# An encoder kernel: the DRAM sums of the second value set, begun in the first layer's second branch half and issued one per 22 matmul steps instead of 15

## The chip, the cores and the metric

The kernel runs on one core of a Trainium2 chip. A core has five engines with a queue of instructions each: TensorE (PE: matmuls; PEld: their weight loads), VectorE (DVE), ScalarE (ACT), GpSimd (POOL) and SyncE (SP). Data move between DRAM and the on-chip memory by 16 DMA engines, which all queues share; here SyncE and GpSimd issue nearly all transfers. The metric is the device time of one execution in microseconds. Lower is better.

## The reference

A two-layer encoder over 272 tokens (16 learned ones and 256) with 2048 channels, in float32. Cut to what matters:

```python
for i in range(DEPTH):                                   # 2 layers
    h = _rmsnorm(h_stream, norm_mix[i])
    proj = h @ w_in[i]                                   # q | k | v | f | ga | gf
    ...
    a_br = attn @ w_attn_br[i]                           # attention branch
    s_br = fr.reshape(B, L, FOURIER_WIDTH) @ w_four[i]   # Fourier branch
    merged = g_attn * a_br + g_four * s_br               # sigmoid gates
    h_stream = h_stream + merged @ w_out[i]
    h2 = _rmsnorm(h_stream, norm_ffn[i])
    up = h2 @ w_up[i]
    u_gate = _dwconv3_centred(up[..., :D_FF], w_conv[i], b_conv[i])
    u_val = up[..., D_FF:]
    h_stream = h_stream + (jax.nn.silu(u_gate) * u_val) @ w_down[i]
return h_stream[:, N_META:]
```

## The kernel before

**Weights come in chunks.** Every weight matrix is read in chunks of 512 KB (128 partitions, 4 tiles of 256 columns). `order` lists all matmul groups in the order in which TensorE runs them, and `chunks` their chunks. `load_raw` (L233) issues one chunk's load on SyncE's queue into a `raw` buffer; there are four (`RAW`, L231). `split_w` (L270) splits a chunk into a rounded high part `wh`, on ScalarE (L277), and the rest `wl`, on VectorE (L279), three buffers each. A matmul with float32 accuracy is then three matmuls: high weights with the high and the low part of the activations, low weights with the high part (L348 to L350). `advance` (L245) issues loads up to four chunks ahead of the newest chunk that is to be split, and splitting runs two chunks ahead of TensorE (`LOOK`).

**Steps.** `group` (L322) runs one group: two output tiles of 128 channels, 2 to 11 chunks. After every second pair of weight tile and output tile, so four times a chunk, it calls `step` (L290), which lets one piece of other work be emitted between the matmuls, and `pump` (L257), which emits one pending split. `four_group` (L364) does the same for the s groups, whose two chunks take eight steps together.

**Branch halves.** Each layer computes the gated branches in two halves of 1024 channels. `BRANCH_ORDER` (L68) sets the order of the groups: ga and gf are the gate projections (16 steps each), s is the Fourier branch and a the attention branch (8 steps each). The second half's order is s4 a4 ga5 gf5 s5 a5 ga6 gf6 s6 a6 ga7 gf7 s7 a7. After each half come eight groups of the output projection (ps_o, 8 steps each). In the first layer an s chunk is first folded by `fold_w` (L264): VectorE writes sums and differences of its tiles into `wpm`, of which there is one buffer, and the split works from that (L267). In the second layer these folds come ready from DRAM (`fw`).

**What the second layer's feed-forward stage needs.** It computes part of the value projection and of the down projection by products of sums (fewer multiplications at the price of sums of weight tiles). The sums of weights lie in DRAM: `fv[0]` and `fv[1]` for two value sets, `ft` for the down projection. They are made in two ways. `prepare` (L509) runs in the first layer's feed-forward stage: GpSimd loads tiles, VectorE adds them, GpSimd stores them; it makes `fw`, `fv[0]` and `ft`. `weight_sums` (L549) makes `fv[1]` without VectorE, by transfers from DRAM to DRAM on GpSimd's queue: a plain copy of 1 MB into `fv[1]`, then a transfer that adds a second 1 MB to it (`accum_op=ALU.add`, called accumulating below). There are four kinds of sums with four blocks each, so 16 plain and 16 accumulating transfers; within a kind the order is copy 0, copy 1, add 0, copy 2, add 1, copy 3, add 2, add 3. Kind 1 copies what kind 0 made, and kind 3 adds what kind 1 made.

**When these transfers are issued.** `slow` (L288) holds a counter, the generator `weight_sums` and a period. While the period is not 0, each unforced `step` takes one off the counter; at 0 the counter is set to the period and the generator issues its next transfer. Before the transfer GpSimd copies one element of the newest `wl` (the `tick`, L554), so that the transfer isn't issued before that chunk was split. GpSimd executes its queue in order, and its few other instructions stand in the same queue, among them the power function of the norm statistics (`tok`, L489) and the loads and stores of `prepare`. The period is 15 from the fifth group (gf0) of the second layer's first half on.

Of the kernel before, what the change touches and what calls it, by code (L numbers as in the profile page):

```python
# [154 lines left out]
def encoder_kernel(ctx, tc, xT, params, consts, bmat, cfold, csign, w_fl, w_f64c, w_in, w_abr, w_four, w_f64, w_out, w_up, w_down, w_vn, w_dn, w_dt, out):  # L155
# [129 lines left out]
    def push(gen, wait=0):  # L285
        shadow.append([wait, gen])

    slow = [0, None, 0]  # L288
# [22 lines left out]
    def drain():  # L311
        while shadow:
            step(True)
# [42 lines left out]
    def split_w64(l, i):  # L356
        r = wp.tile([64, MG * P], F32, tag="r64", name="r64", bufs=1)
        nc.sync.dma_start(r, w_f64[l, i])
        w = wp.tile([96, MG * P], F32R, tag="w64", name="w64", bufs=2)
        nc.scalar.copy(w[0:64], r)  # L360
        nc.vector.tensor_tensor(w[64:96], r[32:64], w[32:64].bitcast(F32), op=ALU.subtract)
        return w
# [142 lines left out]
    def norm_in(m, goff):  # L505
        norm_split(m, goff)
        norm_sum(m)

    def prepare(pool):  # L509
        tt = lambda *v, **kw: tc.keep_in_program_order(nc.vector.tensor_tensor(*v, **kw))  # L510
        dma = lambda *v: tc.keep_in_program_order(nc.gpsimd.dma_start(*v))
        tile_ = lambda n: pool.tile([P, CW, MG * P], F32, tag="ws", name=n, bufs=7)
        folds = [(w_fl[k], k) for k in range(KT)] + [(w_four[1, j, c], KT + 2 * j + c) for j in range(NG) for c in range(2)]
        sums = []
        for s_, f, wd, nq in ((0, fv[0], w_vn[0], NV), (len(VSETS), ft, w_dn, NQ)):
            for k in range(nq):
                sums += [(wd[h, nq * e + k], (s_, f, q, k)) for h, e, q in ((0, 0, 0), (1, 0, 2), (1, 1, 1), (0, 1, 3))]

        def fold(held, n, j):
            a, o = held[n], tile_(f"wo{n}")  # L520
            for q, op in ((0, ALU.add), (1, ALU.subtract)):
                for c in range(2):
                    half = (lambda t_, e: t_[:, 2 * c:2 * c + 2, e * P:(e + 1) * P]) if j < KT else (lambda t_, e: t_[:, 2 * e + c])
                    tt(half(o, q), half(a, 0), half(a, 1), op=op)
                    yield 1
            dma(fw[j], o)

        def sum_up(held, n, s_, f, q, k):
            x, y = held[n], held[n + (1, -2, 1, -1)[q]]
            for c in (0, 2):  # L530
                tt(x[:, c:c + 2], x[:, c:c + 2], y[:, c:c + 2], op=ALU.add)
                yield 1
            dma(f[q, k], x)
            ready_sums.add((s_, q, k))

        for jobs, ahead, work in ((folds, 2, lambda h, n, to: fold(h, n, to)), (sums, 4, lambda h, n, to: sum_up(h, n, *to))):
            held = {}
            for n in range(len(jobs) + ahead):
                if n < len(jobs):
                    held[n] = tile_(f"wi{n}")  # L540
                    dma(held[n], jobs[n][0])
                left = 7 - n % 4 // 3
                if n >= ahead:
                    for v in work(held, n - ahead, jobs[n - ahead][1]):
                        left -= v
                        yield v
                yield left
# [56 lines left out]
    for l in range(DEPTH):  # L604
        last = l == DEPTH - 1
# [5 lines left out]
        with tc.tile_pool(name=f"mix{l}", bufs=1) as mp:  # L611
# [557 lines left out]
            def gate(kind, i):  # L1169
                ps = group((l, kind, i), xr(lo), W)  # L1170
                th = rt("th")
                boff = 2 * KT * l + (0 if kind == "ga" else KT)
                for m in range(MG):
                    u = th[:, m, lo:T]
                    nc.vector.tensor_tensor(u, ps[m][:, :W], rstdB[:, lo:T], op=ALU.mult)
                    bcol = bgh[:, boff + 2 * i + m:boff + 2 * i + m + 1]
                    nc.scalar.activation(u, u, AF.Tanh, bias=bcol, scale=0.5)
                return th

            tha, thf, w64s = {}, {}, []  # L1180
            for half in range(2):
                mH = mL = None
                for n_, (kind, i) in enumerate(BRANCH_ORDER[half]):
                    if last and (half or n_ >= 4):
                        slow[2] = 15
                    j = i - 4 * half
                    if kind == "ga":
                        tha[i] = gate("ga", i)
                    elif kind == "gf":
                        w64s.append(split_w64(l, i))  # L1190
                        thf[i] = gate("gf", i)
                    elif kind == "s":
                        def s_evac(m, ps, th=thf[i]):
                            e, o = (mp.tile([P, TH], F32, tag=t, name=t) for t in ("se", "so"))
                            for a, p_ in ((e, ps[0]), (o, ps[1])):
                                nc.scalar.copy(a, p_[:, TH:2 * TH])
                                nc.vector.tensor_tensor(a, p_[:, :TH], a, op=ALU.add)  # L1197
                            sp = mp.tile([P, T], F32, tag="sp", name="sp", bufs=2)
                            nc.vector.tensor_tensor(sp[:, 0:TH], e, o, op=ALU.add)
                            nc.vector.tensor_tensor(sp[:, TH:T], e[:, T - TH:0:-1], o[:, T - TH:0:-1], op=ALU.subtract)  # L1200
                            t_ = th[:, m, lo:T]
                            nc.vector.scalar_tensor_tensor(t_, t_, 1.0, sp[:, lo:T], op0=ALU.add, op1=ALU.mult)

                        four_group((l, "s", i), fr, x64, w64s.pop(0), s_evac)
                    else:
                        if mH is None:
                            drain()
                            mHf = mp.tile([P, AHn], F32R, tag="aH", name="mH")
                            mLf = mp.tile([P, ALn], F32R, tag="aL", name="mL")
                            mH = mHf[:, :8 * T].rearrange("p (k t) -> p k t", k=8)  # L1210
                            mL = mLf[:, :8 * T].rearrange("p (k t) -> p k t", k=8)
                        ps = group((l, "a", i), lambda kt: (qH[kt // 4][:, kt % 4, lo:T], qL[kt // 4][:, kt % 4, lo:T]), W)
                        for m in range(MG):
                            k = 2 * j + m
                            t_, h_ = tha[i][:, m, lo:T], mH[:, k, lo:T]
                            nc.vector.scalar_tensor_tensor(t_, t_, 1.0, ps[m][:, :W], op0=ALU.add, op1=ALU.mult)
                            nc.vector.tensor_tensor(t_, t_, thf[i][:, m, lo:T], op=ALU.add)
                            nc.scalar.copy(h_, t_)
                            nc.vector.tensor_tensor(mL[:, k, lo:T], t_, h_.bitcast(F32), op=ALU.subtract)
                for mg in range(8):  # L1220
                    ps = group((l, "o", half, mg), lambda kt: (mH[:, kt, lo:T], mL[:, kt, lo:T]), W)
                    for m in range(MG):
                        mt = 2 * mg + m
                        nc.vector.scalar_tensor_tensor(XT[:, mt, lo:T], ps[m][:, :W], 0.5, XT[:, mt, lo:T], op0=ALU.mult, op1=ALU.add)
                        if half == 1:
                            norm_in(mt, P_NF + l * KT)


        with tc.tile_pool(name=f"ffn{l}", bufs=1) as fp:
            hold = {}  # L1230
            push(norm_stats(hold), 8)
            if not last:
                push(prepare(fp), 8)
            def conv_gate(i):
                ps = group((l, "ug", i), xr(lo), W)
# [327 lines left out]
```

## Time and profile before

| what | us |
|---|---|
| median of 3 runs | 2531.81 |
| lowest and highest of them | 2531.63, 2534.08 |
| the profiled execution | 2533.09 |
| its span, from the first instruction to the last | 2531.2 |

The profile is of one execution. Its page gives busy times by engine, a chain of work that ended last, and groups of instructions; the trace behind it can be asked for single instructions, for busy times in stretches of the span, for what an engine waited for, and for the time from a DMA's issue to its landing. Names such as ps_gf<-xHL,wh say what an instruction writes and reads, L348 is a line of the kernel. Matmuls overlap one another, so PE counts as busy nearly always, and its idle time counts more than its share.

The main stages in this trace, by their first instructions: the first layer's second branch half runs from about 370 to 540 us, its feed-forward stage to about 1320, and the 32 transfers of `weight_sums` are issued from 1502 to 1843, in the second layer's branch halves. The second layer's feed-forward stage follows to the end.

### The profile page before, as it was taken

How to read it: one execution, taken by the hardware profiler on the slowest of the kernel's cores; microseconds unless marked ns; L12 is line 12 of the kernel's file. 1: busy time of each engine (PE TensorE's matmuls, PEld its weight loads, DVE VectorE, ACT ScalarE, POOL GpSimd, SP SyncE). 2: the span in 40 equal slices, each digit the busy share in tenths (PEclk: the TensorE clock that was granted, in tenths of full speed). 3: DMA queues.
4: the chain of work that ended last, by engine and by line, in shares of the span. 5: the costliest groups of instructions: out<-in, count | busy, mean ns of one | idle time of the engine just before them, and what ended most of it. 6: DMA issues, size and time to landing. Idle time of an engine off the chain costs nothing.

```text
span 2531.2 us, 47928 instructions
## 1 busy us (share of the span) xinstructions
PE 2517.9 (99%) x18848; PEld 2434.5 (96%) x18848; DVE 1985.4 (78%) x3151; ACT 1343.3 (53%) x1921; POOL 205.9 (8%) x393
## 2 busy tenths in 40 slices
PE   9999999999999999999999999999999999999999
PEld 8999999999999999999999999999988889998887
DVE  7687866778878667888768877666878787898898
ACT  5455434554444334444445555444676675666665
POOL 0000000002212222222200000000100000000000
PEclk9999999999999999999999999999999999999999
DMA  6544555569999999999975648999988887788897
GB/s 238 164 151 160 193 176 187 186 236 371 393 330 377 392 386 376 384 379 386 372 287 184 199 172 250 294 281 307 288 275 295 295 289 240 259 281 289 278 301 270
DMA packets 194770, 706.85 MB, mean 279 GB/s; under 512 B 22112, under 2 KB 27360, under 8 KB 194288
## 3 DMA queue, kind: packets, MB, share of 16 engines
q1 hardware_dynamic: 146768, 517.09, 58.4%
q0 software_dynamic: 46336, 184.57, 21.0%
q8 instruction: 147, 2.41, 0.4%
q10 hardware_dynamic: 1440, 2.13, 0.2%
q14 instruction: 79, 0.65, 0.1%
HBM read 623.32 MB, written 111.15 MB: 290 GB/s over the span
## 4 chain that ended last, share of the span: by engine, by line
PE 96%; DMA 2%; DVE 1%; ACT 1%; issue 0%; SPq 0%; POOL 0%; ACTq 0%; DVEq 0%
PE ps_p L1403 14%; PE ps_ug L350 7%; PE ps_ug L349 7%; PE ps_ug L348 7%; PE ps_d L349 4%; PE ps_uv L349 4%; PE ps_d L348 3%; PE ps_uv L350 3%; PE ps_d L350 3%; PE ps_uv L348 3%; PE ps_o L349 2%; PE ps_gf L349 2%; PE ps_o L348 2%; PE ps_gf L348 2%; PE ps_o L350 2%; PE ps_gf L350 2%
## 5 line engine op out<-in xcount | busy, mean ns | idle before, releaser
L279 DVE TENSOR_TENSOR wl<-raw,wh 128x1024 fp32r<-128x1024 f32 (+1 forms) x961 | 1158.4, 1217 | 411.9 <-ACT wh L277 399.6
L277 ACT CAST wh<-raw 128x1024 fp32r<-128x1024 f32 (+1 forms) x961 | 999.8, 1045 | 901.7 <-PE ps_ug L349 213.3
L349 PE MATMUL ps_ug<-xHL,wh 128*128 128x272 f32 (+1 forms) x1408 | 401.5, 285 | 0.0
L348 PE MATMUL ps_ug<-xHL,wh 128*128 128x272 f32 (+1 forms) x1408 | 400.8, 285 | 0.0
L350 PE MATMUL ps_ug<-xHL,wl 128*128 128x272 f32 (+1 forms) x1408 | 400.4, 286 | 0.1
L349 PEld LDWEIGHTS ps_ug<-xHL,wh 128*128 128x128 f32 x1408 | 264.7, 188 | 3.2
L348 PEld LDWEIGHTS ps_ug<-xHL,wh 128*128 128x128 f32 x1408 | 264.6, 188 | 3.2
L350 PEld LDWEIGHTS ps_ug<-xHL,wl 128*128 128x128 f32 x1408 | 264.0, 188 | 1.5 <-DVE wl L279 1.1
L1403 PE MATMUL ps_p<-wh,opnd 128*128 128x512 f32 x816 | 222.8, 393 | 0.0
L349 PE MATMUL ps_uv<-xHL,wh 128*128 128x272 f32 x704 | 203.3, 289 | 0.0
L349 PE MATMUL ps_d<-gHL,wh 128*128 128x272 f32 x704 | 202.9, 288 | 0.0
L348 PE MATMUL ps_d<-gHL,wh 128*128 128x272 f32 x704 | 202.9, 288 | 0.0
L350 PE MATMUL ps_uv<-xHL,wl 128*128 128x272 f32 x704 | 202.6, 288 | 0.0
L348 PE MATMUL ps_uv<-xHL,wh 128*128 128x272 f32 x704 | 202.3, 287 | 0.0
L350 PE MATMUL ps_d<-gHL,wl 128*128 128x272 f32 x704 | 202.1, 287 | 0.0
L1403 PEld LDWEIGHTS ps_p<-wh,opnd 128*128 128x128 f32 x816 | 148.4, 188 | 29.6 <-ACT wh L277 0.2
L348 PE MATMUL ps_gf<-xHL,wh 128*128 128x272 f32 (+1 forms) x512 | 146.8, 287 | 1.5 <-DVE so L1197 1.5
L348 PE MATMUL ps_ga<-xHL,wh 128*128 128x272 f32 (+1 forms) x512 | 147.9, 289 | 0.1
L510 DVE TENSOR_TENSOR wi<-wi,wi 128x512 f32<-128x512 f32 x224 | 147.0, 685 | 0.0
L349 PE MATMUL ps_o<-mL,wh 128*128 128x272 f32 (+1 forms) x512 | 146.5, 286 | 0.0
L350 PE MATMUL ps_ga<-xHL,wl 128*128 128x272 f32 (+1 forms) x512 | 146.1, 285 | 0.4 <-DVE wl L279 0.4
L349 PE MATMUL ps_ga<-xHL,wh 128*128 128x272 f32 (+1 forms) x512 | 146.1, 285 | 0.0
(378 smaller groups left out, 5967.6 us busy)
## 6 DMA issues: line engine op xcount, KB each, us to landing
raw<-in_w_up SPq DMA_DIRECT2D x288, 512.0 KB, 6.2
raw<-in_w_in SPq DMA_DIRECT2D x191, 512.0 KB, 3.8
raw<-in_w_down SPq DMA_DIRECT2D x88, 512.0 KB, 7.2
wi<-in_w_dn POOLq DMA_DIRECT2D x80, 512.0 KB, 9.6
ft<-wi POOLq DMA_DIRECT2D x80, 512.0 KB, 7.9
raw<-ft SPq DMA_DIRECT2D x80, 512.0 KB, 4.7
raw<-in_w_out SPq DMA_DIRECT2D x64, 512.0 KB, 4.3
raw<-fv SPq DMA_DIRECT2D x64, 512.0 KB, 4.8
```

What stands on the lines that cost most here:

```text
L277: nc.scalar.copy(h[:, a:b], r[:, a:b])
L279: nc.vector.tensor_tensor(lo[:, a:b], r[:, a:b], h[:, a:b].bitcast(F32), op=ALU.subtract)
L348: nc.tensor.matmul(o, h[:, c, sl], a, start=kt == 0, stop=False)
L349: nc.tensor.matmul(o, h[:, c, sl], b, start=False, stop=False)
L350: nc.tensor.matmul(o, lo[:, c, sl], a, start=False, stop=kt == nk - 1)
L510: tt = lambda *v, **kw: tc.keep_in_program_order(nc.vector.tensor_tensor(*v, **kw))
L1403: nc.tensor.matmul(ps[h], x, w[:, 512 * h:512 * h + 512], start=fresh and (s_, q) in BEGIN and first, stop=(s_, q) in END and end, skip_gr ...
```

## The change

```diff
@@ -1181,8 +1181,8 @@
             for half in range(2):
                 mH = mL = None
                 for n_, (kind, i) in enumerate(BRANCH_ORDER[half]):
-                    if last and (half or n_ >= 4):
-                        slow[2] = 15
+                    if half or last and n_ >= 4:
+                        slow[2] = 22
                     j = i - 4 * half
                     if kind == "ga":
                         tha[i] = gate("ga", i)
@@ -1230,6 +1230,7 @@
             hold = {}
             push(norm_stats(hold), 8)
             if not last:
+                slow[2] = 0
                 push(prepare(fp), 8)
             def conv_gate(i):
                 ps = group((l, "ug", i), xr(lo), W)
```

The period is set from the beginning of the second branch half in both layers, and from the fifth group of the first half in the second layer as before. It is 22 steps instead of 15. When the first layer's feed-forward stage begins, the period is set to 0, which stops the transfers until the second layer's fifth branch group. The transfers themselves, their order and everything else are unchanged.

## The prediction

> **What bounds the kernel now.** I read the page's head first, then busy times by stretches, then what the weight loads of TensorE waited for, then single instructions around those waits.
>
> ```profile
> span 2531.2 us, 47928 instructions
> PE 2517.9 (99%) x18848; PEld 2434.5 (96%) x18848; DVE 1985.4 (78%) x3151; ACT 1343.3 (53%) x1921; POOL 205.9 (8%) x393
> ```
>
> TensorE is busy for all but 2531.2 - 2517.9 = 13.3 us. The change touches no matmul, so it can win only idle time that the transfers cause now, and can lose only by making new idle time. The next view gives both places. Its rows are: first layer, second branch half (366 to 545); the first layer's feed-forward stage (545 to 1320); the stretch of the second layer in which all 32 transfers run (1500 to 1845); and two parts of that. Columns: stretch, its length, busy us of PE, PEld, DVE, ACT and POOL (instructions), granted clock, DMA share, GB/s.
>
> ```profile
> 366.00:545.00 179.00, 179.00 (x1435) 178.92 (x1434) 131.70 (x215) 89.00 (x135) 2.71 (x4) 1.00 0.55 183
> 545.00:1320.00 775.00, 775.00 (x6185) 775.00 (x6184) 609.42 (x931) 335.10 (x419) 152.07 (x285) 1.00 0.97 370
> 1500.00:1845.00 345.00, 342.04 (x2838) 340.42 (x2837) 238.57 (x418) 178.46 (x284) 32.23 (x65) 1.00 0.88 280
> 1576.00:1608.00 32.00, 29.45 (x241) 28.79 (x240) 22.89 (x42) 15.81 (x28) 4.04 (x7) 1.00 0.92 282
> 1608.00:1672.00 64.00, 64.00 (x536) 64.00 (x535) 39.28 (x57) 25.07 (x29) 6.29 (x14) 1.00 0.91 286
> ```
>
> The place that receives transfers (first row) has a full TensorE and a DMA share of only 0.55. The place that gives them up has 0.88, and TensorE lacks 345.00 - 342.04 = 2.96 us there. A high DMA share alone doesn't do it: at 0.97 nothing is lost in the second row. The loss is local, 2.55 us of it in the 32 us of the fourth row, while the 64 us after it, at the same share, lose nothing. TensorE's instructions at the gaps (start, duration, idle time before and its releaser in brackets):
>
> ```profile
> 1599.50 0.40 PE L383 MATMUL ps_s<-fr,wh 128*128 128x276 f32 x1
> 1600.76 0.33 PE L384 MATMUL ps_s<-fr,wl 128*128 128x138 f32 x1 [0.86 <-DVE wl L279]
> ...
> 1603.67 0.28 PE L389 MATMUL ps_s<-x,w 96*128 96x138 f32 x1
> 1605.40 0.38 PE L348 MATMUL ps_gf<-xHL,wh 128*128 128x258 f32 x1 [1.46 <-DVE so L1197]
> ...
> 1687.37 0.28 PE L349 MATMUL ps_ga<-xHL,wh 128*128 128x258 f32 x1
> 1688.07 0.39 PE L350 MATMUL ps_ga<-xHL,wl 128*128 128x258 f32 x1 [0.41 <-DVE wl L279]
> ```
>
> From start to start these three take 1.26, 1.73 and 0.70 us. Neighbours follow at 0.12 to 0.19 us, so the stalls are about 1.1 + 1.6 + 0.6 = 3.3 us. What the DMAs did before them, in GpSimd's rows:
>
> ```profile
> 1577.32 0.89 POOL L555 DMA_DIRECT2D fv<-in_w_vn  x1
> ...
> 1585.57 0.89 POOL L555 DMA_DIRECT2D fv<-in_w_vn  x1 [0.81 <-issue]
> ...
> 1594.20 0.52 POOL L555 DMA_DIRECT2D fv<-fv  x1
> ...
> 1608.82 0.51 POOL L555 DMA_DIRECT2D fv<-fv  x1
> ...
> 1660.90 0.88 POOL L555 DMA_DIRECT2D fv<-in_w_vn  x1 [0.90 <-issue]
> ...
> 1671.81 0.89 POOL L555 DMA_DIRECT2D fv<-in_w_vn  x1 [0.26 <-issue]
> ...
> 1678.55 0.52 POOL L555 DMA_DIRECT2D fv<-in_w_vn  x1
> ```
>
> At the stalls issues are 8.3, 8.6 and 6.7 us apart. From 1608.82 to 1660.90 there are five intervals of 10.4 us on average, and no stall. How long one is under way (KB, median us to landing; accumulating ones show their size, plain copies don't):
>
> ```profile
> fv<-in_w_vn POOLq DMA_DIRECT2D x12, 1024.0 KB, 11.9
> ...
> fv<-in_w_vn POOLq DMA_DIRECT2D x12, 7.7
> ```
>
> So at both places one transfer was issued while an accumulating one (about 12 us) still ran. What that does to the weight loads (last row of the answer on raw; min/median/max to landing) for loads issued from 366 to 545, from 1617.1 to 1629 (after one accumulating transfer, issued at 1617) and from 1672 to 1681.5 (after the overlapping pair):
>
> ```profile
> DMA to landing us min/median/max: 3.1/3.3/6.7
> ...
> DMA to landing us min/median/max: 6.5/7.9/9.8
> ...
> DMA to landing us min/median/max: 9.3/11.1/12.3
> ```
>
> A single accumulating transfer stretches loads from 3.3 to at most 9.8 us and TensorE didn't notice (1608 to 1672 above); a pair stretches them to 12.3, and it did. That overlap is the bound to be argued about.
>
> **The change part by part.** (1) Counting. A gate group takes 16 steps (4 chunks of 4), each s, a and o group 8. The second half of a layer has 4 s, 4 a, 3 ga, 3 gf and 8 o groups: 32 + 32 + 48 + 48 + 64 = 224 steps. In the first layer, one per 22 from step 1 makes transfers at steps 1, 23, ... 221: 11 of 32, six plain and five accumulating. Three steps remain after the last, so 19 remain on the counter when the second layer resumes it; the other 21 come at steps 19, 41, ... 459, where before the 32nd came at 1 + 31 x 15 = 466. The last transfer is thus no later than now.
>
> (2) Spacing in the second layer. First and last issue before:
>
> ```profile
> 1502.12 0.56 POOL L555 DMA_DIRECT2D fv<-in_w_vn  x1
> ...
> 1843.43 0.95 POOL L555 DMA_DIRECT2D fv<-fv  x1 [0.30 <-issue]
> ```
>
> 341.3 us over 31 intervals is 11.0 us, or 0.734 us a step; 22 steps are 16.1 us on average. Single intervals now go down to 6.7 us (above), 4.3 under the mean, because an issue waits for the newest split chunk. With the same scatter the shortest will be 16.1 - 4.3 = 11.8: a 12 us transfer is just over. The DMA load: without transfers I take the first layer's 0.55, raised by 272/258 columns to 0.58. The 32 transfers then cost (0.88 - 0.58) x 345 / 32 = 3.2 us of all 16 engines each. Afterwards the second layer has 0.58 + 21 x 3.2 / 345 = 0.77. Removed of the 3.3 us: between 0 (every stall stays) and 3.3. The nearest row is 1608 to 1672, whose issues stand 10.4 us apart and lose nothing; I take 3.0, since one close pair may remain.
>
> (3) The first layer's half: 0.55 + 11 x 3.2 / 179 = 0.75 of the DMA engines, below the 0.97 that costs nothing. The tightest place there is the folded chunks of the s groups, which the second layer doesn't have. For s5 (SyncE's two issues, DVE, first matmul on the second chunk):
>
> ```profile
> 390.46 3.29 SPq L240 DMA_DIRECT2D raw<-in_w_four  x2
> ...
> 402.48 1.29 DVE L267 TENSOR_TENSOR wpm<-raw 128x512 f32<-128x512 f32 x2
> 404.97 1.23 DVE L279 TENSOR_TENSOR wl<-wpm,wh 128x1024 fp32r<-128x1024 f32 x1 [1.19 <-ACT wh L277]
> ...
> 406.94 0.34 PE L383 MATMUL ps_s<-fr,wh 128*128 128x276 f32 x1
> ```
>
> The second load is issued at 390.46 + 3.29 - 0.33 = 393.4 (an issue takes 0.33) and may land until 402.48, 9.1 us later, as its fold waits for the one wpm buffer anyway. Its split ends at 406.20, so TensorE has 0.7 us left: the limit is 9.8 us. Plain transfers and single accumulating ones stay at or under that; only an overlapping pair (12.3) would cost 12.3 - 9.8 = 2.5 us. By my count of steps, the transfers nearest to s loads are plain ones (steps 23, 67 and 111), the accumulating ones meet ga, gf, a and o loads, so I take 0.2, between 0 and 3 x 2.5 = 7.5 (s5 to s7; the loads of s4 are issued before step 1).
>
> (4) GpSimd gets 11 ticks and issues of some 0.2 + 0.9 us in the first layer. It has nothing else there:
>
> ```profile
> 541.22 0.85 POOL L489 TENSOR_TENSOR tok<-ms,mhalf 128x3 f32<-128x3 f32 x1 [376.34 <-DVE ms L585]
> ```
>
> It sat idle for 376 us before this norm statistic. The eleventh transfer comes three steps before the end of the half, and the statistic eight steps into the next stage: 11 x 0.734 = 8 us apart, so it should be issued near 533. If it came late, the statistic would wait about 1.1 us; the first up-gate group's 16 steps cover that. Its target's base copy was issued 44 steps earlier, so it needs no wait. SyncE's queue gets nothing. Cost 0; the preparation queued behind it on GpSimd starts when the statistic has, as before. Setting the period to 0 in the feed-forward stage keeps transfers out of the row with 0.97.
>
> Sum: -3.0 + 0.2 = **-2.8 us**: span 2531.2 to 2528.4, the profiled execution 2533.09 to 2530.3. The median of the runs is 2531.81, 1.3 below the profiled one; from it 2529.0.
>
> A rule bears on step 3. The Trainium skill, "DMA: Bandwidth & Descriptors", section "Queues, rings and completion order", says that each DMA engine alternates between queues that have work, a packet at a time. By that rule and equal packets a load beside a transfer would need about twice 3.3 us, 6.6, and no s group could ever be late. The rows of this trace (9.8 after one accumulating transfer) speak against equal packets. The packets:
>
> ```profile
> DMA packets 194770, 706.85 MB, mean 279 GB/s; under 512 B 22112, under 2 KB 27360, under 8 KB 194288
> ...
> q8 instruction: 147, 2.41, 0.4%
> q14 instruction: 79, 0.65, 0.1%
> ```
>
> 482 packets are of 8 KB or more; 226 are instruction loads, which leaves 256 = 16 x 16, for 16 accumulating transfers of 1 MB: 64 KB each. Such a packet holds up a load however far apart the transfers stand, so the five accumulating ones in the first layer will stretch loads there just as in the second.
>
> **The rivals.** (B) The stalls stay: in the second layer's stretch of s and a groups, where chunks are used up faster, a single accumulating transfer may do for the stall. For it: 2.55 of the 2.96 us fell into that stretch, and a single one stretches loads to 9.8 us. Against it: no gap follows one from 1608 to 1672. Time: 2531.8.
>
> (C) Slower: the folded s chunks of the first layer are late. It decides where a second s load takes over 9.8 us; then each of s5 to s7 loses up to 2.5 us, 7.5 in all, against -3.0: +4.5, 2536.3. For it: 9.8 is exactly the worst landing after a single accumulating transfer. Against it: by the count of steps the accumulating ones fall elsewhere, if issues don't drift.
>
> (D) More gain: the second layer's feed-forward stage starts with late splits, too.
>
> ```profile
> PEld ps_uv L345 <- DVE wl L279: 0.7, 1, 0.7
> ...
> PEld ps_ug L350 <- DVE wl L279: 0.5, 1, 0.5
> ```
>
> If these 1.2 us were owed to the last transfers, they could go too: 2529.0 - 1.2 = 2527.8. Against it: ScalarE and VectorE are dense there, and the last transfer moves by 7 steps only.
>
> **How the numbers follow.** Forecast 0.58, its own range 2528 to 2530.5; B 0.16; C 0.15; D 0.11. 0.2% is 5.1 us, about what a measurement of this kernel tells from no change. The forecast and B lie within it. C passes it only if nothing is gained or more than s is late: 0.10. D passes it only with another loss found: 0.06. So faster 0.06, same 0.84, slower 0.10. Range: 2526.5 (D less the 1.3 us between the median and the profiled execution) to 2535 (most of C).
>
> **What would show it.** Right: 11 issues between 372 and 535, 21 from about 1515 to 1840, intervals over 11 us; TensorE at 179 of 179 in the first row and above 344.5 of 345 in the third; the two waits at 1600 and 1605 gone. Wrong: TensorE waiting on wl in ps_s or ps_ga between 366 and 545 (C); gaps in the second layer's s groups with transfers 15 us apart (B); or a time off by more than 4 us, which nothing counted here explains, such as another order of the instructions on DVE or ACT.

## The result, and the profile after

| | before | after |
|---|---|---|
| median, us (22 runs each) | 2533.80 | 2529.78 |
| lowest and highest | 2531.38, 2537.77 | 2527.26, 2532.27 |
| the profiled execution, and its span | 2533.09, 2531.2 | 2531.8, 2529.8 |

The ratio is 0.9981, with a 95% interval of 0.9975 to 0.9987: 4.8 us won by the ratio (3.3 to 6.3), 4.0 by the medians. A second comparison of the unchanged two kernels (`after_again` below) gave 0.9980 [0.9971, 0.9989]. The sign and the place are as predicted; the gain is larger than the 2.8 us of the sum. The profiled execution of after lies 2.0 us above the median of its kernel, so its trace understates the gain. One execution of a kernel below (`half14`, 6352.40 us) counts as slow and is left out of its ratio.

First the head of after's page, then its busy times in the stretches that the prediction used (stretch, length, busy us of PE, PEld, DVE, ACT and POOL, granted clock, DMA share, GB/s).

```profile
span 2529.8 us, 47935 instructions
PE 2517.8 (100%) x18848; PEld 2435.4 (96%) x18848; DVE 1985.4 (78%) x3151; ACT 1343.6 (53%) x1921; POOL 205.2 (8%) x393
```

```profile
366.00:545.00 179.00, 179.00 (x1434) 178.92 (x1434) 131.57 (x215) 89.07 (x136) 12.95 (x26) 1.00 0.79 247
545.00:1320.00 775.00, 775.00 (x6185) 775.00 (x6184) 609.51 (x931) 335.07 (x419) 152.62 (x285) 1.00 0.98 370
1500.00:1845.00 345.00, 342.94 (x2846) 341.46 (x2844) 239.59 (x419) 180.00 (x287) 20.69 (x43) 1.00 0.79 250
1576.00:1608.00 32.00, 29.94 (x247) 29.41 (x246) 22.76 (x42) 15.82 (x28) 1.79 (x4) 1.00 0.83 267
1608.00:1672.00 64.00, 64.00 (x537) 64.00 (x535) 39.19 (x58) 25.56 (x29) 3.56 (x8) 1.00 0.80 246
```

The first row has taken in eleven transfers (POOL 12.95 us against 2.71, DMA share 0.79 against 0.55) and TensorE is as full as before. The third row has lost eleven, but TensorE still lacks 2.06 us of 345, all of it in the fourth row. What GpSimd issued, and TensorE's instructions at the gaps that remain:

```profile
372.20 0.71 POOL L555 DMA_DIRECT2D fv<-in_w_vn  x1
...
529.93 0.92 POOL L555 DMA_DIRECT2D fv<-in_w_vn  x1
541.18 0.88 POOL L489 TENSOR_TENSOR tok<-ms,mhalf 128x3 f32<-128x3 f32 x1 [10.34 <-DMA raw<-in_w_up]
...
1569.43 0.90 POOL L555 DMA_DIRECT2D fv<-in_w_vn  x1 [0.89 <-issue]
1586.97 0.90 POOL L555 DMA_DIRECT2D fv<-in_w_vn  x1 [0.26 <-issue]
1601.58 0.52 POOL L555 DMA_DIRECT2D fv<-in_w_vn  x1 [0.27 <-issue]
```

```profile
1599.79 0.40 PE L383 MATMUL ps_s<-fr,wh 128*128 128x276 f32 x1 [0.77 <-ACT wh L277]
1601.05 0.33 PE L384 MATMUL ps_s<-fr,wl 128*128 128x138 f32 x1 [0.86 <-DVE wl L279]
...
1604.66 0.38 PE L348 MATMUL ps_gf<-xHL,wh 128*128 128x258 f32 x1 [0.42 <-DVE so L1197]
```

The issues at 1569.43 and 1586.97, before the gaps, are accumulating ones, 17.5 us apart, and land in 11.4 and 14.3 us: they do not overlap. So the place of the loss was read rightly, and its condition (two transfers at once) was not. That is where the experiments begin.

### The profile page after: what moved, and what is told of

Its sections match the earlier page's. It is cut to its first block, busy times and chain, and to the rows that moved or that the text cites. A ratio compares the mean times of both kernels' runs of the same rounds, so it can differ in the third digit from the quotient of the medians.

```text
span 2529.8 us, 47935 instructions
## 1 busy us (share of the span) xinstructions
PE 2517.8 (100%) x18848; PEld 2435.4 (96%) x18848; DVE 1985.4 (78%) x3151; ACT 1343.6 (53%) x1921; POOL 205.2 (8%) x393
## 4 chain that ended last, share of the span: by engine, by line
PE 97%; DMA 1%; DVE 1%; ACT 0%; issue 0%; SPq 0%; DVEq 0%; ACTq 0%
PE ps_p L1404 14%; PE ps_ug L350 7%; PE ps_ug L349 7%; PE ps_ug L348 7%; PE ps_d L349 4%; PE ps_uv L349 4%; PE ps_d L348 3%; PE ps_uv L350 3%; PE ps_d L350 3%; PE ps_uv L348 3%; PE ps_o L349 2%; PE ps_o L348 2%; PE ps_o L350 2%; PE ps_gf L349 2%; PE ps_gf L348 2%; PE ps_gf L350 2%
## 5 line engine op out<-in xcount | busy, mean ns | idle before, releaser
L350 PE MATMUL ps_o<-mH,wl 128*128 128x272 f32 (+1 forms) x512 | 146.1, 285 | 0.0
```

Source lines behind the costliest of these rows:

```text
L350: nc.tensor.matmul(o, lo[:, c, sl], a, start=False, stop=kt == nk - 1)
```

## The experiments

A yardstick for all of them. The chunks are split in the same order in every kernel, so the end of the same split on VectorE can be compared: one in the second layer's first gf groups, before its first s group (1523.7 us in the profile of before), and one behind the last of these gaps, in the output projection of the second half (1794.4). The last five transfers of before, and the last three of after, are issued behind it. Columns: how far each profiled execution is behind (+) or ahead of (-) the first profile of before, us, and the difference.

```
kernel          at 1523.7   at 1794.4   won between
after             -0.17       -1.45        1.3
after_again       -0.30       -2.95        2.7
half14            -0.15       -2.79        2.6
early15           +0.19       -3.37        3.6
none              -1.24       -5.28        4.0
ticks_only        +0.25       -3.86        4.1
plain             +0.32       -3.79        4.1
plain15           -0.45       -4.62        4.2
gates16           -0.57       -4.73        4.2
wide23            +6.01       +1.91        4.1
first7           +44.46      +40.36        4.1
before_again      +1.23       +3.83       -2.6
before_third      +0.17       +2.79       -2.6
```

Seven kernels win 4.0 to 4.2 us there, which is the floor of this stretch: the first profile of before lost 4.1 us in it, not the 3.3 that the prediction summed from three gaps.

**No transfers at all** (`none`), and ticks without transfers (`ticks_only`). Both leave out the sums of the second value set: its products read weight tiles in their place.

```diff
-    vprods = [{... 3: f[3], 4: f[0], 5: f[1], 6: f[2]} for i, f in enumerate(fv)]
+    vprods = [{... 3: f[3], 4: f[0], 5: f[1], 6: f[2]} for i, f in enumerate((fv[0], [w_vn[1, 0, 0:NV]] * 4))]
...
-    slow[1] = weight_sums()
+    ready_sums.update((1, q, k) for q in range(4) for k in range(NV))
```

> None of the 32 transfers is issued; the products of the second value set read the weight tiles themselves in place of their sums, so those sums are left out of the computation. It gives the floor: what all 32 transfers cost wherever they stand. Both theories: TensorE has no idle time between 1500 and 1845 us (the changed kernel's profile still lacks 2.06 us there, the one before 2.96), and the time is some 2 us below the changed kernel and 5 to 6 us below the one before (ratio 0.9977 to 0.9981). If the stalls there were not owed to these transfers, it would equal the changed kernel.

`ticks_only` has the first edit, and in place of the second it drops the DMA behind the tick:

```diff
-            tc.keep_in_program_order(nc.gpsimd.dma_start(out_, s, **kw))
```

> The changed kernel without any of the 32 transfers, but with the 32 one-element copies on GpSimd kept, and with them their small on-chip tile; the sums of the second value set are left out, as in the run without transfers. That run had no stall between 1500 and 1845 us, yet its matmuls followed one another more slowly from 1860 us on (235 ns from start to start of the 512-column ones, 227 in all other runs). If the missing tile did it by shifting the tiles behind it, the 227 ns come back here and the time is the floor: 2529.0 to 2529.5 us where the kernel before has 2534 (ratio 0.998), within 1 us of the changed kernel and of the one with plain copies. If the other source of the loads did it, 235 ns stay and the time is 2532 again.

Measured: `none` 2532.12, ratio 0.9990 [0.9981, 0.9999]; `ticks_only` 2528.76, ratio 0.9980 [0.9971, 0.9989]. In `none` TensorE is full from 1500 to 1845 but for 0.3 us:

```profile
1500.00:1845.00 345.00, 344.71 (x2855) 342.99 (x2855) 241.87 (x423) 182.78 (x292) 0.85 (x1) 1.00 0.57 185
```

and yet it loses 3.2 us to before later, after 1862, with no waits. The groups of TensorE there, in `none` and then in `ticks_only` (busy us, mean ns):

```profile
L1404 PE MATMUL ps_p<-wh,opnd 128*128 128x512 f32 x804 | 221.8, 396 | 0.0
```

```profile
L1403 PE MATMUL ps_p<-wh,opnd 128*128 128x512 f32 x808 | 220.5, 393 | 0.0
```

From start to start, where two of the first row follow each other, they take 234.6 ns on average in `none` and 232.6 in after and `ticks_only`; 235 and 227 are only the most common values. With the tick tile and its copies back, and still no transfers, the pace is back. So `none` measures two things, and `ticks_only` is the clean one: without any transfer the ratio is 0.9980, with after's timing of them 0.9981. Each interval is 0.0006 to 0.0009 wide to either side, up to 2.3 us, so the times show nothing that better timing could still bring; the yardstick still has after's two profiles 2.8 and 1.4 us behind the floor.

**Period 15 in both places** (`early15`), and one per 14 steps in the second half of each layer alone (`half14`: sixteen transfers in each layer, none between 1500 and 1665).

```diff
-                        slow[2] = 22
+                        slow[2] = 15
```

> Early start with the old period of 15: 15 transfers in the first layer, 17 in the second, all of these in its first half. Theory of the stretch (a stall is made where transfers, above all accumulating ones, follow closely in the s and a groups of the second layer's first half): that stretch is as dense as before, so 2 to 3 us of idle TensorE remain at about 1600 us and only what fell later is won; the time is 0.5 to 1.5 us below the one before (ratio 0.9994 to 0.9998). Theory of the load (what counts is how many transfers run in the second layer): with 17 instead of 21 there it is at least as fast as the changed kernel (ratio 0.9981 or less).

```diff
-                    if half or last and n_ >= 4:
-                        slow[2] = 22
+                    if half:
+                        slow[2] = 14
```

> Transfers in the second branch halves alone, 16 in each layer, one per 14 steps. Theory of the stretch: with none in the second layer's first half the stall at 1600 us goes; what may come are stalls where two overlap, as intervals fall to about 10 us: TensorE lacks under 1 us in 1500 to 1845, the time is 1 to 2 us below the changed kernel (ratio 0.9973 to 0.9979). Theory of the load: 16 in the second layer, but packed into its second half at the old density, so it loses there what it wins before: about the changed kernel (0.9981) or up to 2 us above. The rival of late folded s chunks in the first layer: TensorE waits in ps_s between 366 and 545 us, up to 2.5 us a group, and the time is above the one before.

Measured: `early15` 2530.12, 0.9980 [0.9970, 0.9990]; `half14` 2531.00, 0.9984 [0.9975, 0.9993]. Neither differs from after beyond the intervals. In the first layer's half TensorE stays at 178.99 and 179.00 us of 179, with DMA shares of 0.86 and 0.89: fifteen and sixteen transfers there cost as little as eleven. The idle 2 to 3 us that `early15` was expected to keep near 1600 did not come: it has one gap there, of 0.41 us at 1602.74, although its transfers stand as close as before's. `half14`, which has no transfer near 1600, has no gap there either, but one of 1.26 us at 1777 (ps_o waiting for mL): a loss is possible outside that place as well. It follows a single accumulating transfer, issued at 1761.02: the load issued at 1763.29 took 9.6 us to land (3.8 in `plain15` below), its split came late, and in VectorE's queue mL stands behind that split.

**All 32 as plain copies**, with the change's timing (`plain`) and with that of before (`plain15`).

```diff
-                        issue(dst(q, j - 1), more(j - 1), accum_op=ALU.add, max_dma_last_dim=4096)
+                        issue(dst(q, j - 1), more(j - 1))
```

> The changed kernel with its 16 accumulating transfers turned into plain copies to the same place (the second addend overwrites the first, so the sums of the second value set are left out). Number, place and written bytes are the same. If a single accumulating transfer makes what is left of the stall at 1600 us: loads issued in 1500 to 1845 land in at most 8 us (now 10.5), TensorE lacks under 0.5 us there (now 2.06), and the time is that of the kernel without transfers, 2 us below the changed one (ratio 0.997 to 0.998). If any transfer of 1 MB does it: no change against the changed kernel (ratio 0.9981).

`plain15` has this edit in the kernel before. Both leave the sums of the second value set undone. The edit takes away two things, the addition and the limit `max_dma_last_dim=4096`.

> The kernel before (all 32 transfers in the second layer, one per 15 steps) with its 16 accumulating transfers turned into plain copies to the same place; the sums of the second value set are left out. Theory of the accumulating transfers (they alone stretch the loads, plain ones are over too soon): TensorE lacks under 0.5 us from 1500 to 1845, the time is 4 to 5 us below the kernel before (ratio 0.998 to 0.9985) with no change of place or pace. Theory of the number (32 transfers of 1 MB in the second layer are too many at any kind): at least half of the loss stays, TensorE lacks over 1.5 us there, the ratio is above 0.999.

Measured: `plain` 2529.29, 0.9974 [0.9963, 0.9986]; `plain15` 2529.29, 0.9981 [0.9972, 0.9990]. Both are at the floor. `plain15` has as many transfers as before, at before's distance, and moves as many bytes to the same places:

```profile
1500.00:1845.00 345.00, 344.70 (x2857) 343.10 (x2856) 242.13 (x422) 182.66 (x293) 24.39 (x65) 1.00 0.80 283
```

So it isn't their number, and not their distance as such: the accumulating ones, as this kernel issues them, do it. The DMA queues from 1500 to 1845 show how the two differ (q0 carries the transfers; packets, MB, share of 16 engines), first of before, then of `plain15`:

```profile
DMA packets 22373, 96.49 MB, mean 280 GB/s; under 512 B 2496, under 2 KB 2816, under 8 KB 22084
...
q0 software_dynamic: 4592, 32.51, 36.8%
```

```profile
DMA packets 18835, 97.61 MB, mean 283 GB/s; under 512 B 2525, under 2 KB 2845, under 8 KB 18290
...
q0 software_dynamic: 1021, 33.56, 24.3%
```

A plain copy takes 24.3% x 345 / 32 = 2.6 us of all 16 engines. Before has 31 transfers whole in this window (32.51 MB), 16 of them plain: the other 15 take (36.8% x 345 - 16 x 2.6) / 15 = 5.7 us each, 2.2 times as long (the expectation of `first7` below has 7.2, which is too much). Packets of 8 KB and over: 22373 - 22084 = 289 against 18835 - 18290 = 545. Sixteen copies more bring 256 large packets more, so the plain copies have the packets of 64 KB, and an accumulating transfer has (4592 - 256 - 509) / 15 = 255 small ones, where 509 = 1021 - 512 is what else the queue carries. Spread over 1 MB, that is 4 KB a packet, the limit in its call. Whether the addition does the harm or the small packets do is open: a plain copy in packets of 4 KB was not run. The Trainium skill, "DMA: Bandwidth & Descriptors", section "Queues, rings and completion order", has the engines change queues at packet boundaries; by that alone the large packets should hold a load up more, and this trace doesn't bear it out, since the transfers with the small packets do the harm.

**The first layer overloaded**: one per 7 steps from its second half on (`first7`), and one per 23 from the start of its first half (`wide23`).

```diff
-                    if half or last and n_ >= 4:
-                        slow[2] = 22
+                    if half:
+                        slow[2] = 7
```

> All 32 transfers in the first layer's second branch half, one per 7 steps (5.2 us); none in the second layer. It takes away the room that the change uses. From the changed kernel's packets an accumulating transfer takes 7.2 us of all 16 DMA engines and a plain one 2.8, on average 5.0: with 0.55 for the loads the demand is 1.5 of what there is. The rival of late folded s chunks, at its strongest: TensorE waits in the first layer in ps_s, ps_a and ps_ga, 5 to 30 us in all, and the time is above the kernel before (ratio 1.000 to 1.010). If the first layer hides transfers in any number, the time is the floor, 2529 us.

```diff
-                    if half or last and n_ >= 4:
-                        slow[2] = 22
+                    if half or not last:
+                        slow[2] = 23
```

> The transfers spread over both branch halves of the first layer and the second half of the second, one per 23 steps, so that none stands in the second layer's first half, where the changed kernel's profile still has its stalls (1598 to 1604 us). If those are the rest of the loss: TensorE lacks under 0.5 us from 1500 to 1845, nothing in the first layer, and the time is that of the kernel with plain copies, 0.5 to 1 us below the changed kernel (ratio 0.9974 to 0.9979). If another load in the first half of the first layer, where the norm of keys and queries and the attention run beside, is late for it, TensorE waits between 150 and 366 us.

Measured: `first7` 2573.86, 1.0160 [1.0146, 1.0174]; `wide23` 2534.99, 1.0003 [0.9993, 1.0012]. In `first7` (rows of its stretches, then what the weight loads waited for from 366 to 545: total, times, longest):

```profile
366.00:545.00 179.00, 152.39 (x1134) 149.29 (x1133) 99.85 (x161) 65.76 (x98) 28.28 (x54) 0.93 0.94 291
545.00:700.00 155.00, 151.13 (x1188) 149.07 (x1187) 124.27 (x231) 75.14 (x105) 29.07 (x54) 1.00 0.99 349
```

```profile
PEld ps_gf L350 <- DVE wl L279: 16.8, 6, 7.3
PEld ps_gf L348 <- ACT wh L277: 6.3, 3, 5.0
```

The half that absorbs sixteen transfers for nothing doesn't absorb all 32. TensorE lacks 26.6 + 3.9 us, and the granted clock of 0.93 takes up to another 0.07 x 179 = 12.5: 43 of the 44.5 us that it is behind. The gate groups starve, not the folded s chunks. `wide23` is at its floor in the second layer and loses 6 us in the first layer's first half:

```profile
290.00:310.00 20.00, 16.40 (x120) 16.19 (x119) 10.82 (x17) 7.02 (x11) 0.70 (x2) 0.91 0.75 257
```

The wait is that of ps_a for wl, 3.8 us, in the s and a groups of the first half, as near 1600 in the second layer. Two accumulating transfers stand before it, issued at 264 and 283. In these runs the place of the transfers decides, and how close they stand there; their number alone does not.

**Transfers out of the s and a groups of the second layer** (`gates16`), with both kernels run again beside it.

```diff
-                    if half or last and n_ >= 4:
-                        slow[2] = 22
+                    if last:
+                        slow[2] = 16 if n_ >= 4 * (1 - half) and kind[0] == "g" else 0
+                    elif half:
+                        slow[2] = 14
...
+                if last:
+                    slow[2] = 16
                 for mg in range(8):
```

> All 32 transfers as in the changed kernel's design, but placed by groups: one per 14 steps in the first layer's second half (16 of them, as in half14), and in the second layer one per 16 steps in the ga, gf and o groups alone, none issued during s and a groups. If s and a groups are where a single accumulating transfer hurts (my revised theory), the stretch 1500 to 1845 should be at its floor, 4 us or more ahead of the profile of before, with no wait on wl in ps_s or ps_a; median at or below after_again by 0 to 1 us. If transfers still under way when an s group begins do the harm as well, or if o and gate groups suffer at 12 us distance, there is no difference from after_again (2529.8), or up to 2 us more.

> The changed kernel again, unaltered, for a second profile on the chip on which gates16 runs. If its stalls in the second layer come and go between executions (a single accumulating transfer meets an s or a load or doesn't), this profile shows between 0 and 3 us lost from 1500 to 1845, at other places than the first one's 1598 to 1604, and the median stays within 1 us of 2529.8. If they are fixed by the order of the work, the same three gaps return.

> The kernel before again, unaltered, for a second profile. By the theory that overlapping and single accumulating transfers delay loads at chance, it loses 3 to 6 us from 1500 to 1860 against the floor of plain15, at gaps that need not be those of the first profile. If the loss is fixed by the order, the same three gaps of 1.26, 1.73 and 0.70 us return near 1600, 1605 and 1688.

Measured: `gates16` 2528.78, 0.9979 [0.9970, 0.9988]; `after_again` 2529.85, 0.9980 [0.9971, 0.9989]; `before_again` 2536.92. `gates16` is at the floor and has no wait on wl in ps_s or ps_a; its median is 1.1 us under the changed kernel's, too little to call it faster. Laid beside after, it explains what happens there. The same three events in both: SyncE's issues of the two chunks of an s group, and ScalarE's part of the second one's split. First after, then `gates16`:

```profile
1586.42 0.33 SPq L240 DMA_DIRECT2D raw<-fw  x1
...
1589.43 0.33 SPq L240 DMA_DIRECT2D raw<-fw  x1
...
1598.69 1.04 ACT L277 CAST wh<-raw 128x1024 fp32r<-128x1024 f32 x1 [4.77 <-DMA raw<-fw]
```

```profile
1583.01 0.33 SPq L240 DMA_DIRECT2D raw<-fw  x1
...
1586.01 0.33 SPq L240 DMA_DIRECT2D raw<-fw  x1
...
1594.93 1.05 ACT L277 CAST wh<-raw 128x1024 fp32r<-128x1024 f32 x1 [1.51 <-DMA raw<-fw]
```

and the landings (min/median/max) of the loads issued from 1570 to 1577, then from 1585.5 to 1591, first the two of after, then the two of `gates16`:

```profile
DMA to landing us min/median/max: 9.0/10.1/10.5
...
DMA to landing us min/median/max: 3.1/9.2/9.3
```

```profile
DMA to landing us min/median/max: 4.3/4.7/4.9
...
DMA to landing us min/median/max: 7.6/8.2/8.8
```

The second chunk takes about 9 us to land in both, because both have an accumulating transfer at that moment (issued at 1586.97 and 1582.96), and both splits wait for it. But after issues its load 3.4 us later, and splits it 3.8 us later. An earlier accumulating transfer (1569.43) had stretched the three loads issued right behind it to 9 to 10.5 us, their splits came late, and with four raw buffers the next loads could not be issued until those were split. `gates16` has one accumulating transfer in this stretch, after has two, 17.5 us apart: the first uses up the lead, the second meets loads that have none. `wide23` has the same pattern, two of them 19 us apart. The moment at which the second chunk lands orders the kernels as their losses do: `gates16` at 1594.8 (nothing lost against the floor), `early15` 1596.7 (0.5 us), `after_again` 1597.1 (1.4), after 1598.6 (2.8).

So much for this place. No run takes out the first of the two transfers alone, and the pattern is no general rule: three more pairs in after (issued at 466 and 481, 1693 and 1708, 1814 and 1832) cost nothing, and in `half14` one accumulating transfer was enough.

**Where before loses the rest.** `before_again` waits in the same places as the first profile, but has lost 2.6 us more by 1794. Its idle time accounts for 1.0 (341.00 busy of 345, against 342.04). The rest is in the granted clock:

```profile
1595.00:1605.00 10.00, 6.80 (x55) 6.43 (x54) 3.55 (x6) 3.97 (x6) 0.02 (x1) 1.00 0.86 318
...
1605.00:1612.00 7.00, 7.00 (x48) 7.00 (x48) 6.87 (x15) 4.04 (x10) 1.50 (x2) 0.76 0.58 193
...
1606.00:1608.00 2.00, 2.00 (x10) 2.00 (x10) 1.97 (x7) 1.26 (x3) 0.00 (x0) 0.50 0.43 135
```

Behind stalls of 2.34 and 0.86 us the clock falls to half; (1 - 0.76) x 7 = up to 1.7 us are lost. A third profile of before put this to the test.

> The kernel before, unaltered, a third profile. My theory now: its extra time over the first profile (typical span 2533.5 against 2531.2) is a granted clock that falls to half for some 3.4 us (1.7 us lost) right behind a stall of TensorE near 1600, which 56 of 74 executions show as a mean clock of 0.999 or 0.998. If so, this execution either shows a mean clock of 1.000, a span of 2528 to 2531.5 and no stretch under 1.00 from 1590 to 1700, or 0.999, a span of 2532 to 2536 and a stretch near 0.5 behind a stall over 2 us there. The rival: the clock dips lie elsewhere (the start, the first layer) and the time from 1500 to 1845 is as in the first profile.

Measured: 2536.03, span 2534.1, mean clock 0.999. Its stalls near 1600, and its clock behind them:

```profile
1600.40 0.40 PE L383 MATMUL ps_s<-fr,wh 128*128 128x276 f32 x1 [1.19 <-ACT wh L277]
1601.66 0.48 PE L384 MATMUL ps_s<-fr,wl 128*128 128x138 f32 x1 [0.86 <-DVE wl L279]
```

```profile
1601.00:1603.00 2.00, 1.34 (x6) 1.34 (x7) 1.93 (x5) 1.25 (x2) 0.00 (x0) 0.65 0.69 229
1603.00:1605.00 2.00, 2.00 (x11) 2.00 (x11) 2.00 (x5) 0.77 (x3) 0.00 (x0) 0.50 0.61 211
1605.00:1607.00 2.00, 2.00 (x11) 2.00 (x11) 1.86 (x7) 1.05 (x1) 0.00 (x0) 0.50 0.79 260
1607.00:1609.00 2.00, 2.00 (x13) 2.00 (x13) 1.45 (x2) 1.69 (x4) 0.69 (x2) 0.64 0.11 25
1609.00:1611.00 2.00, 2.00 (x19) 2.00 (x18) 1.90 (x7) 0.16 (x1) 0.00 (x0) 1.00 1.99 764
```

The dip is at the same place, twice as long as expected, behind shorter stalls than expected. By the clock up to (0.35 + 0.50 + 0.50 + 0.36) x 2 = 3.4 us are lost; the yardstick has 2.6 more than in the first profile, with as much idle time (342.20 busy of 345). The mean granted clock of every run tells how common this is:

```
clock     before: runs, mean span    after: runs, mean span
1.000       18    2530.1               32    2527.8
0.999       46    2533.5                1    2528.9
0.998       10    2535.1                0
all         74    2532.9               33    2527.8
```

(Before: the runs beside the first eleven experiments; after: its own 22 and the 11 of `after_again`.) Between the spans at clock 1.000 lie 2.3 us, between all of them 5.1. So nearly half of the gain is there without any dip, the stalls themselves; the other 2.8 us go with executions whose clock dips, which after hardly has. That these dips sit behind the stalls near 1600 is shown in the two profiles of before that have one; that it is so in the 56 runs of the table is inferred. For it: `wide23`, which stalls elsewhere, shows a clock under 1.000 in 10 of 11 runs. Against its being all: the five kernels at the floor that have no such stall in their profiles (`none`, `ticks_only`, `plain`, `plain15`, `gates16`) show it in 7 of 51.

## Why the prediction was right, and where not

**Place and sign: right.** It named the stretch of the second layer as the one that can win and the first layer's second half as the one that pays nothing. Both hold: first row 179.00 of 179, and `early15` and `half14` show that fifteen and sixteen transfers pay nothing there either.

**Counting (step 1): right.** Eleven issues from 372 to 530, 21 in the second layer, the last at 1832, and intervals of 12 to 19 us there.

**Overlap as the bound (steps 2 and 3): wrong.** "That overlap is the bound to be argued about" and "a 12 us transfer is just over" led to 3.0 of 3.3 us removed. With no two transfers overlapping, after's first profile still lost 4.1 - 1.3 = 2.8 us against the floor, its second 1.4. The prediction's own signs say the same: TensorE was to be above 344.5 of 345 and the waits at 1600 and 1605 gone, but it was at 342.94, with three waits between 1599 and 1605; and gaps in the s groups with transfers 15 us apart were the sign that it gave for B. The bound near 1600 is the lead of the weight loads: two accumulating transfers within some 20 us use it up one after the other. This is rival B's mechanism with a second transfer added to it (without one at 1777 in `half14`), and B's time (nothing won) is wrong as well, since a third and two thirds of the loss went in these two profiles.

**The size of the stall term: too small twice.** Three gaps gave 3.3 us; the floor shows 4.1. Two shorter waits of before's weight loads, which the sum left out, make up most of the difference:

```profile
PEld ps_s L383 <- ACT wh L277: 0.3, 1, 0.3
PEld ps_ga L348 <- DVE so L1197: 0.3, 1, 0.3
```

And the profiled execution of before was one of the better ones: its clock was 1.00 throughout, while 56 of 74 executions show a dip. The median of three, 2531.81, shared this luck; over 22 runs it is 2533.80. The sum of 2.8 fits the 2.3 us between executions at full clock, and what it lacks are the 2.8 us that go, on average, with executions whose clock dips: the clock itself, and in part longer stalls (1.0 of 2.6 us in `before_again`). The predicted 2529.0 lies 0.8 under the measured median, because too low a starting point (by 2.0) and too small a gain (by 1.2) cancelled in part. That is luck.

**Cost in the first layer (rival C): didn't happen.** Loads there took at most 9.3 us:

```profile
DMA to landing us min/median/max: 3.1/4.5/9.3
```

The limit of 9.8 was worked out for the second load of an s group, and the loads of s5 to s7 took at most 5.5 us: the accumulating transfers met other loads, as the count of steps had said, so the limit was never reached. In `gates16` the second load of s5 (issued at 392.92) took 9.7 us, just under it, and nothing was lost (179.00 of 179); the longest load there, 12.1 us, belongs to a gate group. Overload does come, but at one transfer in 7 steps and in the gate groups.

**GpSimd's queue (step 4): right.** The norm statistic starts at 541.18, as before (541.22), 11 us after the last transfer's issue.

**Engine time of a transfer: a mean of two different things.** 3.2 us each gave DMA shares of 0.75 and 0.77; measured are 0.79 and 0.79. With 2.6 for a plain and 5.7 for an accumulating one, the first layer's half gives 0.55 + (6 x 2.6 + 5 x 5.7) / 179 = 0.80. The prediction put the 64 KB packets to the accumulating transfers; they are the plain copies'.

**More gain (rival D): its source was wrong.** The two waits at the start of the feed-forward stage are still there:

```profile
PEld ps_uv L345 <- DVE wl L279: 0.8, 1, 0.8
...
PEld ps_ug L350 <- DVE wl L279: 0.4, 1, 0.4
```

They stay in `none` too, so no transfer makes them.

## What to carry to other kernels

A background transfer is harmful where the loads' lead is short, and the lead can be used up by a chain of loads: look at the transfer before the last one, and at the loads that wait for buffers, and not only at whether transfers overlap. Short stalls of TensorE can cost twice, once as idle time and once as a halved clock behind them, so a single profile at full clock gives too little for what removing them is worth. Compare the profiled execution's clock with those of all runs before taking it as typical.

## What the runs showed of the hardware that was not expected

- TensorE's granted clock went to 0.50 behind stalls of 1.19 and 0.86 us within 2.5 us (`before_third`), and behind 2.34 and 0.86 (`before_again`); behind 0.86 and 1.46 within 5 us (the first profile of before) and 0.77 and 0.86 (after) it stayed at 1.00. The Trainium skill, "TensorE: Matmul & The Clock Gate", section "Part 1: The HAM clock gate", puts the fall to half rate after an idle window of about 3.4 us. The half clock here lasts about 3.4 and 6.8 us, one and two such windows, and agrees with it; but no stall was 3.4 us long.
- An accumulating transfer of 1 MB from DRAM to DRAM, in packets of 4 KB, took 5.7 us of all 16 engines, a plain copy of the same size in packets of 64 KB 2.6, and in these runs only the first kind stalled this kernel.
- The pace of 512-column matmuls was 234.6 ns in `none` and 232.6 in `ticks_only` on average. What differs between them is the tick tile and its copies, so where tiles lie in on-chip memory may matter; what lies where was not looked at.
